# First output projection: four operands loaded and split during the heads, the first result in a tile of its own, the second early sum row loaded 26 matmuls later

## The chip, the core and the metric

The kernel runs on one core of one Trainium2 chip. A core has TensorE (PE, matrix products into PSUM banks), VectorE (DVE), ScalarE (ACT), GpSimd (POOL) and SyncE (SP, which issues DMA transfers and waits for their conditions). The engines run at the same time and wait for each other by semaphores; each one takes its own instructions in order. The metric is device time in microseconds (us) of one execution.

## What is computed

One decoder layer on 1024 tokens of width 1024 in float32. The parts that matter here, cut from the reference:

```python
u = x * (1.0 + sc1) + sh1
proj = u @ w_in[l]
qa, ka, va, dq, dk, dv, z, b_raw, a_raw, g_a, g_b = _split_in(proj)
y_a = _sliding_window_attention(qa, ka, va, sinks[l]) @ w_oa[l]
y_b = _gated_deltanet(dq, dk, dv, z, b_raw, a_raw, ...) @ w_ob[l]
mixed = (jax.nn.sigmoid(g_a) * y_a + jax.nn.sigmoid(g_b) * y_b) @ w_out[l]
x = _layer_norm(ALPHA * x + (1.0 + gt1) * mixed, ln1_g[l], ln1_b[l])
...
```

The window attention has 16 heads. The gated delta rule has 8 heads of 128 channels, each a chain over 8 blocks of 128 tokens. "The first output projection" is the product with `w_oa`. Behind the layer norm follows a squared-ReLU MLP.

## The kernel before

**Products.** Every large float32 product runs as three products of rounded parts: an operand is split into a high part (ACT copies it into a rounded type) and a low part (DVE subtracts the high part from the source). A split costs one instruction on ACT and one on DVE (helper `split_s`, lines 218 to 220: the copy at 219, and `lag` matmuls later the subtraction at 220).

**Order.** The order of PE, ACT and DVE is written out by hand. `at(p, f)` puts a step at matmul number `p`, `after(n, f)` puts it `n` matmuls behind the current one; `count[0]` counts the large matmuls, and before each of them `run_events` emits the steps that are due. `vec` and `act` do the same but move a step into windows that the chain of a head leaves free. SP and POOL are not in this order: a planner places their transfers by when tiles and data are ready in its own reckoning, and each of the two queues then runs in that order and waits at its head.

**Stages.** `Q0` (line 685) is where the heads of the delta rule begin: 24 units of 48 matmuls (line 1436: products for q, v and the gate `gb`) run from `Q0` to `OA` (line 1328, 1152 matmuls later), and the steps of the heads stand between these matmuls. Head `h` runs from `R0 + 120 h`, with `R0 = Q0 + 160` (line 960): `hd_load` brings its matrices, `hd_z` (line 1131) and `hd_x` (1141) complete the inverse of its triangular blocks from the tiles L21 and T1 (`hd_solved`, 1089), and `hd_a`, `hd_b`, `hd_c` are the chain. `hd_x` of a head also runs `hd_z` of the next one into the same bank. `hd_norm` and `hd_out` (1261, 1281) finish a head and store it in `og_d`.

**The sums for the projection.** The projection is a seven-product scheme on quarters (Winograd's form of Strassen's), done for pairs of feature blocks. Its moving operands are the quarters 11, 21 and 22 of the attention output (`attn_d`) and the sums T1 to T4 (`at_d`). The rows of sums are made from `attn_d` by `ts_load`, four steps `ts_step` on DVE (line 1340) and two stores. Rows 0 and 1 are made early (`ts_early`, line 1349) in the two `gate` tiles of `gpool`, rows 2 and 3 near the end of the heads in four tiles of the pool `pc` (`ts_late`). Behind row 1, `ada_open` takes the two gate tiles for loads of `w_ada` (line 1040), 64 of them, each with an add on DVE.

**Operands.** `q_load` (1371) brings half an operand into a raw tile, `q_split` (1379) splits it into a tile named by `HOME`. Operands 11 and T2 are loaded at the end of the heads into the four tiles `late`; the other five (`REST`, line 1433) come through three raw tiles `or` of the pool `p2`, which `open_p2` (1461) opens at `OA + 8` in the space of the pools `pc` and `pce`: it can be used only when all that was in them is done, the last head's store in `og_d` included. `o_load`, `o_op` and `o_sum` (1390 to 1416) bring blocks of `w_oa`, form the sums of these that the seven products need, and split them, at the places of the list `OPS` (1420).

**Projection.** Line 1544 runs 28 products of 12 matmuls from `OA`: for the pairs 0 and 1 in the order 1, 6, 7, 4, then 2, 5, 3, and for the pairs 2 and 3 the other way round. Products 1, 6, 7 and 4 of a pair add up in one bank (`mm`), and so do 5 and 3 (`b`). What stands in a bank between two products is copied out by ACT (`o_part`, line 1506) or added to an earlier copy by DVE (`o_full`, line 1511), before PE may go on in that bank. The copies are in tiles `t` of `p2` (six of them, line 1500); each is stored to `ta_d` by POOL when it is complete, and then its tile is free. `y_load` (1518) fetches them again for the next stage.

Of the kernel before, what the change touches and what calls it, by code (L numbers as in the profile page):

```python
# [9 lines left out]
F32 = mybir.dt.float32  # L10
# [7 lines left out]
P = 128  # L18
D = 1024
S = 1024  # L20
KT = D // P  # L21
NT = S // P
HALF = 512
# [11 lines left out]
def hybrid_layer_kernel(ctx: ExitStack, tc: tile.TileContext,  # L35
                        x, c, w_ada, b_ada, w_in, conv_w, a_log, dt_bias, sinks, dn_norm_w,
                        w_oa, w_ob, w_out, ln1_g, ln1_b, w_ff1, b_ff1, w_ff2, b_ff2,
                        ln2_g, ln2_b, out, dbg=None):
    nc = tc.nc
    x, c, out = x[0], c[0], out[0]  # L40
# [160 lines left out]
    def at(p, f, *args):  # L201
        order[0] += 1
        heapq.heappush(events, (p, order[0], f, args))

    def after(n, f, *args):
        at(count[0] + n, f, *args)
# [728 lines left out]

    pce_pool = tc.tile_pool(name="pce", bufs=1)
    pce = pce_pool.__enter__()
    pc = pc_pool = None
    TTs = []

    def open_pc():
        nonlocal pc, pc_pool
        pb_pool.__exit__(None, None, None)
        vhl_pool.__exit__(None, None, None)
        kp_pool.__exit__(None, None, None)
        pc_pool = tc.tile_pool(name="pc", bufs=2, side="right")
        pc = pc_pool.__enter__()
        for i in range(2):
            TTs.append(pc.tile([P, NT, P], F32, name=f"TT{i}", bufs=1))
            V.memset(TTs[i][64:128, :, 0:64], 0.0)  # L950
# [27 lines left out]
    def vec(lag, cost, f, *args):  # L978
        q = window("V", count[0] + lag, cost)
        at(q, f, *args)  # L980
        return q
# [67 lines left out]
    def ada_load(i, f, k):  # L1049
        w, lo = ada["w"][i % 3], ada_cols_of(f)  # L1050
        nc.sync.dma_start(out=w, in_=w_ada[k * P:(k + 1) * P, lo:lo + HALF])
        q = vec(36, 3.3, ada_add, w, k)
        if k == KT - 1:
            at(q + 7, ada_part, f)

# [26 lines left out]
        after(4, put)  # L1082

    items = [(f, k) for f in range(KT) for k in range(KT)]
    at(Q0 + 112, ada_open)
    for i, (f, k) in enumerate(items):
        at(Q0 + 120 + 14 * i, ada_load, i, f, k)

    def hd_solved(h):
        d = heads[h]  # L1090
# [204 lines left out]
    def gb_done(i):  # L1295
        ts = []

        def done(half, pt):
            t = big4("gz", shape=[P, HALF])
            A.activation(out=t, in_=pt, func=AF.Copy)  # L1300
            nc.sync.dma_start(out=gb_d[i, :, halves[half]], in_=t)
        return done

    for h in range(8):
# [23 lines left out]
    OA = L0 + 48  # L1328
# [20 lines left out]
    def ts_early(k):  # L1349
        tiles = [gpool.tile([P, S], F32, tag="gate", name="ts") for _ in range(2)]  # L1350
        ts_load(k, tiles)
        after(22, ts_step, k, tiles, 0)

    late = []

# [4 lines left out]
            vec(22 + 14 * i, 3.3, ts_step, 2 + i, late[2 * i:2 * i + 2], 0)  # L1360

    at(Q0 + 6, ts_early, 0)
    at(Q0 + 58, ts_early, 1)
    at(R0 + 7 * PER + 2, ts_late)

    QUAD = {"11": (attn_d, 0, 0), "21": (attn_d, 4, 0), "22": (attn_d, 4, 1),
# [14 lines left out]
        quad[name, j] = [(big, big2)[pool].tile([P, 2, HALF], F32R, tag=f"{c}{i + j}", name="q" + c) for c in "hl"]  # L1381
        split_s(*quad[name, j], qraw[name, j], 5)

    for n, (name, j) in enumerate((a, j) for a in ("11", "T2") for j in range(2)):
        at(OA - 66 + n, lambda name, j, n: q_load(name, j, late[n]), name, j, n)
        at(L0 + 8 + 6 * n, q_split, name, j)

    wraw, wop, opn = {}, {}, [0]

# [14 lines left out]
    def o_sum(i, what):  # L1404
# [10 lines left out]
        else:  # L1415
            sub(V, f2h, f2h, f1l)

    at(L0 - 24, o_load, 0, 0)
    at(L0 - 20, o_load, 0, 1)
    OPS = [(-48, 0, "a0"), (-42, 1, "a0"), (-36, 0, "+b"), (-35, 0, "+g0"), (-30, 1, "+b"), (-29, 1, "+g0"),  # L1420
# [9 lines left out]
    for pair in (2, 3):  # L1430
        at(OA + 97, o_load, 1, pair)

    REST = [(n, j) for n in ("T3", "T4", "21", "T1", "22") for j in range(2)]
    RSPLIT = (30, 34, 38, 56, 60, 64, 80, 84, 88, 104)

    for kind, h in units_h:
        if kind == "q":
# [59 lines left out]
    ot = {}  # L1497

    def o_tile(i, c):
        ot[i, c] = p2.tile([P, HALF], F32, tag="t", name="t", bufs=6)  # L1500
        return ot[i, c]

    def o_put(i, c):
# [14 lines left out]
    def y_load(f):  # L1518
        sg = gpool.tile([P, S], F32, tag="gate", name="sg")
        nc.gpsimd.dma_start(out=sg, in_=gb_d[f])  # L1520
        ga = p2.tile([P, S], F32, tag="or", name="ga", bufs=3)
        nc.gpsimd.dma_start(out=ga, in_=ga_d[f])
        ta = [p2.tile([P, HALF], F32, tag="t", name="ta", bufs=6) for _ in range(2)]
        for half in range(2):
            nc.gpsimd.dma_start(out=ta[half], in_=ta_d[f, :, halves[half]])
        ygate[f] = sg, ga, ta
        after(22, lambda: A.activation(out=ga, in_=ga, func=AF.Sigmoid))
        after(28, lambda: A.activation(out=sg, in_=sg, func=AF.Sigmoid))
        for half in range(2):
            after(30 + 4 * half, lambda half: V.tensor_tensor(out=ta[half], in0=ta[half], in1=ga[:, halves[half]],  # L1530
                                                               op=ALU.mult), half)

    at(OA + 7 * 48 - 24, y_load, 0)

    PRODUCT = {1: ("a0", "11", "A", True), 2: ("a4", "21", "B", True), 3: ("g4", "22", "C", False),
               4: ("b4", "T4", "A", False), 5: ("b0", "T1", "C", True), 6: ("g0", "T2", "A", False),
# [7 lines left out]
    for i, m in turns:  # L1544
        w, mv, ab, begin = PRODUCT[m]
        if begin:
            tag = {"A": "mm", "B": "a", "C": "b"}[ab]
            obank[i, ab] = psum(tag, {"mm": 3, "a": 2, "b": 2}[tag])
        pt = obank[i, ab]
        for k in range(4):  # L1550
            for x_ in range(3):
                run_events(count[0])
                t, (qh, ql) = wop[i, w], quad[mv, k // 2]
                lw, r = ((0, qh), (0, ql), (1, qh))[x_]
                T.matmul(pt, lhsT=t[:, lw, k, :], rhs=r[:, k % 2, :], start=begin and k == 0 and x_ == 0,  # L1555
                         stop=k == 3 and x_ == 2, skip_group_check=True)
                count[0] += 1
        e = count[0] + 1
        c = {1: 0, 2: 0, 6: 1, 3: 1, 7: 3, 5: 3, 4: 2}[m]
        if m == 4:  # L1560
            at(e if i > 1 else OA + (128, 152)[i], o_part, i, c, pt, True)
        else:
            at(e, o_part if (m in (1, 6, 7)) == (i < 2) else o_full, i, c, pt)

# [33 lines left out]
    def open_pe():  # L1598
        nonlocal pe, pe_pool, gt1, parts
        p2_pool.__exit__(None, None, None)  # L1600
        gp_pool.__exit__(None, None, None)
        pe_pool = tc.tile_pool(name="pe", bufs=2, side="right")
        pe = pe_pool.__enter__()
        gt1 = pe.tile([P, D], F32, tag="gx", name="gt1", bufs=1)
        row(gt1, gt_d[0])
        parts = pe.tile([P, NT, 2, 6], F32, name="parts", bufs=1)
        for i, name in enumerate(("11", "21", "22")):
            tiles = [[big2.tile([P, 2, HALF], F32R, tag=f"{c}{2 * i + j}", name=f"u{name}{c}") for j in range(2)]
                     for c in "hl"]
            U[name, "t"] = tiles  # L1610
            U[name] = [[t[k // 2][:, k % 2, :] for k in range(4)] for t in tiles]
        for name, k0, u in (("T1", 0, 1), ("T2", 4, 1), ("T3", 0, 0), ("T4", 4, 0)):
            U[name] = [[t[k0 + k].rearrange("p (j u c) -> p j u c", j=4, u=2)[:, :, u, :] for k in range(4)]
                       for t in (mh, ml)]
# [673 lines left out]
```

## Time and profile before

| what | us |
|---|---|
| median of 3 runs | 1829.96 (1828.35 to 1831.01) |
| the profiled execution | 1830.16 |
| its span, first to last instruction | 1828.5 |
| PE busy in the span | 1791.9 |
| mean granted clock of PE | 0.992 |

A line of the timeline gives start, duration, engine, source line, operation, the tiles written and read, and in square brackets how long the engine had been idle and what released it. Engines with a q are sequencers; SPq lines are issues of DMA transfers. A line of the waits gives who waited for whom: total, times, longest. A line of the windows gives the stretch, its length, the busy time of PE, weight loads (PEld), DVE, ACT and POOL with their instruction counts, the granted clock, the share of the DMA engines and GB/s.

### The profile page before, as it was taken

Reading aid. Unit: us, or ns where it says so; the run is one execution under the profiler, and the core shown is the slowest. Engines: PE = TensorE matmul, PEld = TensorE weight load, DVE = VectorE, ACT = ScalarE, POOL = GpSimd, SP = SyncE. Lnnn points to the kernel's source line nnn. Section 1 sums busy time; section 2 is a strip of 40 time slices with the busy share of each in tenths; the row PEclk is TensorE's granted clock in tenths of the full one; section 3 lists DMA queues with packets and bytes.
Section 4 is the critical chain, followed back from the end, with each engine's and each line's share of the span. In section 5 each row is a group of like instructions: output and inputs, shape, how many; then the busy total and the mean of one; then the engine's idle time right before and its main releaser. Section 6 shows DMA issues by size and latency. Waiting matters only on the chain.

```text
span 1828.5 us, 26402 instructions
## 1 busy us (share of the span) xinstructions
PE 1791.9 (98%) x9136; PEld 1506.9 (82%) x9137; DVE 1300.8 (71%) x2430; ACT 1044.5 (57%) x2363; POOL 318.8 (17%) x482
## 2 busy tenths in 40 slices
PE   8999999999998999999988999999999999999998
PEld 6988888888886888888877888888888888888887
DVE  7688688888855567767567455788777766576697
ACT  4699678888864556555465332466555554434341
POOL 0233234453340011101001210001222220000000
PEclk8999999999999999999999999999999999999999
DMA  9656722232267556565666754358888879855671
GB/s 280 202 199 207 225 67 96 65 111 70 73 221 241 131 181 189 169 184 161 227 215 197 257 167 150 120 163 297 307 290 274 278 274 385 277 184 184 198 263 46
DMA packets 270903, 357.66 MB, mean 196 GB/s; under 512 B 27201, under 2 KB 172306, under 8 KB 270514
## 3 DMA queue, kind: packets, MB, share of 16 engines
q1 hardware_dynamic: 230898, 231.81, 40.2%
q0 software_dynamic: 31728, 107.39, 17.5%
q10 hardware_dynamic: 8144, 16.78, 2.6%
q8 instruction: 72, 1.18, 0.3%
q14 instruction: 61, 0.50, 0.1%
HBM read 242.93 MB, written 110.90 MB: 194 GB/s over the span
## 4 chain that ended last, share of the span: by engine, by line
PE 43%; DVE 2%; DMA 2%; ACT 2%; issue 1%; ACTq 0%; SPq 0%; DVEq 0%; POOLq 0%
PE mm L2149 8%; PE mm L2209 7%; PE mm L262 5%; PE a L2209 4%; PE b L2149 4%; PE b L2209 4%; PE a L2149 3%; PE mm L1778 2%; PE c L2209 2%; PE a L1778 1%; PE mm L1555 1%; PE b L1555 1%; PE c L1778 1%; PE c L2149 0%; DMA or<-at_d 0%
## 5 line engine op out<-in xcount | busy, mean ns | idle before, releaser
L262 PE MATMUL mm<-uh,wh 128*128 128x512 f32 x800 | 320.3, 400 | 0.0
L262 PE MATMUL mm<-uh,wl 128*128 128x512 f32 x800 | 319.8, 400 | 0.0
L262 PE MATMUL mm<-ul,wh 128*128 128x512 f32 x800 | 319.2, 399 | 0.0
L220 DVE TENSOR_TENSOR sp<-sraw,sp 128x1024 fp32r<-128x1024 f32 x112 | 132.7, 1219 | 75.7 <-ACT sp L219 75.7
L219 ACT ACTIVATE sp<-sraw 128x1024 fp32r<-128x1024 f32 x112 | 112.6, 1054 | 120.9 <-PE b L2209 75.4
L262 PEld LDWEIGHTS mm<-uh,wh 128*128 128x128 f32 x800 | 151.0, 189 | 26.5
L262 PEld LDWEIGHTS mm<-ul,wh 128*128 128x128 f32 x800 | 151.1, 189 | 26.2
L262 PEld LDWEIGHTS mm<-uh,wl 128*128 128x128 f32 x800 | 151.1, 189 | 26.1
L2209 PE MATMUL mm<-sp 128*128 128x512 f32 x528 | 135.9, 389 | 0.0
L2209 PEld LDWEIGHTS mm<-sp 128*128 128x128 f32 x528 | 98.8, 188 | 20.4
L2209 PE MATMUL a<-sp 128*128 128x512 f32 x336 | 92.2, 389 | 0.0
L825 DVE CUSTOM_DVE_ANT_0 nscore<-a,amask,nsink 128x256 f32<-128x256 f32 (+1 forms) x128 | 54.5, 463 | 44.8 <-PE a L818 44.5
L1234 ACT ACTIVATE vn<-a,brk 128x128 f32<-128x128 f32 x64 | 23.6, 369 | 99.8 <-PE a L1232 99.7
L2209 PE MATMUL b<-sp 128*128 128x512 f32 (+1 forms) x336 | 79.6, 374 | 0.0
L2209 PEld LDWEIGHTS a<-sp 128*128 128x128 f32 x336 | 63.1, 188 | 13.1
L237 DVE TENSOR_TENSOR wl<-wr,wh 128x1024 fp32r<-128x1024 f32 x56 | 69.0, 1231 | 3.4 <-ACT wh L233 3.4
L836 POOL TENSOR_TENSOR sm<-sm 128x256 f32<-128x256 f32 x56 | 51.5, 919 | 104.8 <-ACT sm L832 73.8
L2209 PEld LDWEIGHTS b<-sp 128*128 128x128 f32 x336 | 60.3, 188 | 11.2
L220 DVE TENSOR_TENSOR wl<-fraw,wh 128x1024 fp32r<-128x1024 f32 x43 | 52.5, 1221 | 19.7 <-ACT wh L219 19.6
L832 ACT ACTIVATE sm<-nscore,stat 128x257 f32<-128x257 f32 (+1 forms) x128 | 62.0, 487 | 2.7 <-DVE stat L825 2.5
L219 ACT ACTIVATE wh<-fraw 128x1024 fp32r<-128x1024 f32 x43 | 44.9, 1054 | 31.0 <-PE b L2149 25.1
L877 POOL TENSOR_SCALAR_AFFINE_SELECT pl<-ph 128x512 fp32r<-128x512 f32 x56 | 53.7, 960 | 41.7 <-DVE ph L870 38.1
(577 smaller groups left out, 4761.2 us busy)
## 6 DMA issues: line engine op xcount, KB each, us to landing
wr<-in_w_in_dram SPq DMA_DIRECT2D x60, 512.0 KB, 3.6
sraw<-hf_d SPq DMA_DIRECT2D x54, 512.0 KB, 4.4
adaw<-in_w_ada_dram SPq DMA_DIRECT2D x74, 256.0 KB, 4.9
fraw<-in_w_ff_dram SPq DMA_DIRECT2D x32, 512.0 KB, 5.1
sraw<-wt_d SPq DMA_DIRECT2D x32, 512.0 KB, 4.5
hf_d<-t ACTq DMA_DIRECT2D x48, 256.0 KB, 3.6
wt_d<-wx POOLq DMA_DIRECT2D x48, 256.0 KB, 4.0
sraw<-in_w_ff_dram SPq DMA_DIRECT2D x22, 512.0 KB, 7.4
```

Source lines behind the costliest of these rows:

```text
L219: A.activation(out=hi, in_=src, func=AF.Copy)
L220: after(lag, lambda: V.tensor_tensor(out=lo, in0=src, in1=hi.bitcast(F32), op=ALU.subtract))
L237: V.tensor_tensor(out=hl[1], in0=raw, in1=hl[0].bitcast(F32), op=ALU.subtract)
L262: T.matmul(ts[half], lhsT=w[:, k, :], rhs=xx[k][:, sl], start=k == 0 and m == 0, stop=k == KT - 1 and m == 2)
L825: V.tensor_tensor_reduce(out=ns[:, i, 1:1 + W], in0=sc[:, i * 2 * P:i * 2 * P + W], in1=amask[:, mo:mo + W], scale=-1.0, scalar=nsink[:, 2 ...
L832: A.activation(out=sm[:, i, 0:1 + W], in_=ns[:, i, 0:1 + W], func=AF.Exp, scale=-1.0, bias=st[:, i:i + 1], accum_out=st[:, 2 + i:3 + i])
L836: G.tensor_tensor(out=sm[:, :, 1 + P:1 + 2 * P], in0=sm[:, :, 1:1 + P], in1=sm[:, :, 1 + P:1 + 2 * P], op=ALU.add)
L877: G.affine_select(out=flat4(part), in_=flat4(full), pattern=[[0, 4], [1 if odd else -1, P]], compare_op=ALU.is_ge if odd else ALU.is_gt, f ...
L1555: T.matmul(pt, lhsT=t[:, lw, k, :], rhs=r[:, k % 2, :], start=begin and k == 0 and x_ == 0, stop=k == 3 and x_ == 2, skip_group_check=True)
L1778: T.matmul(pt, lhsT=m[k][:, tok], rhs=w[:, k % 2, :], start=k == 0 and w is wh and m is mh, stop=k == KT - 1 and m is ml)
L2149: T.matmul(pt, lhsT=a[:, kk, :], rhs=b[k], start=begin and k == 0 and x_ == 0, stop=k == 3 and x_ == 2, skip_group_check=True)
L2209: T.matmul(to, lhsT=a[:, f, t * P:(t + 1) * P], rhs=b[:, f, lo:up], start=(begin or own) and s % NS == 0 and f == 0 and x_ == 0, stop=s % ...
```

## The change

- Row 1 of the early sums is loaded at `Q0 + 84` instead of `Q0 + 58`; its first sum stands 40 matmuls behind that instead of 22, and row 0's 30 instead of 22. `ada_open` and the `w_ada` loads start 56 and 52 matmuls later, 13 matmuls apart instead of 14, with the add 33 behind the load instead of 36.
- The stores of `gb` are issued by ACT instead of SP.
- Operands T3 and T4 are loaded together with 11 and T2, into a tile of `pc` and three of `pce`, and split from `OA - 10` on. The raw tiles of `p2` then bring 21, T1 and 22, split at other places.
- The blocks of `w_oa` for the pairs 0 and 1 are loaded 30 and 32 matmuls earlier; their first sums and splits (a0, b, g0) stand 26 to 39 matmuls earlier, b4 of pair 0 stands 13 earlier.
- A new pool `yo`, opened before `pc`, holds one tile `t0`, for the results (0,0), (0,2), (2,0) and (2,2) one after another; `p2` has five tiles `t` instead of six.
- The copies of product 4 stand at `OA + 150, 176, 326, 346` instead of 128, 152 and right behind the product (325 and 337), and `y_load(0)` 5 matmuls later.

```diff
--- before.py
+++ after.py
@@ -935,14 +935,16 @@
 
     pce_pool = tc.tile_pool(name="pce", bufs=1)
     pce = pce_pool.__enter__()
-    pc = pc_pool = None
+    pc = pc_pool = yo = yo_pool = None
     TTs = []
 
     def open_pc():
-        nonlocal pc, pc_pool
+        nonlocal pc, pc_pool, yo, yo_pool
         pb_pool.__exit__(None, None, None)
         vhl_pool.__exit__(None, None, None)
         kp_pool.__exit__(None, None, None)
+        yo_pool = tc.tile_pool(name="yo", bufs=1, side="right")
+        yo = yo_pool.__enter__()
         pc_pool = tc.tile_pool(name="pc", bufs=2, side="right")
         pc = pc_pool.__enter__()
         for i in range(2):
@@ -1049,7 +1051,7 @@
     def ada_load(i, f, k):
         w, lo = ada["w"][i % 3], ada_cols_of(f)
         nc.sync.dma_start(out=w, in_=w_ada[k * P:(k + 1) * P, lo:lo + HALF])
-        q = vec(36, 3.3, ada_add, w, k)
+        q = vec(33, 3.3, ada_add, w, k)
         if k == KT - 1:
             at(q + 7, ada_part, f)
 
@@ -1082,9 +1084,9 @@
         after(4, put)
 
     items = [(f, k) for f in range(KT) for k in range(KT)]
-    at(Q0 + 112, ada_open)
+    at(Q0 + 168, ada_open)
     for i, (f, k) in enumerate(items):
-        at(Q0 + 120 + 14 * i, ada_load, i, f, k)
+        at(Q0 + 172 + 13 * i, ada_load, i, f, k)
 
     def hd_solved(h):
         d = heads[h]
@@ -1298,7 +1300,7 @@
         def done(half, pt):
             t = big4("gz", shape=[P, HALF])
             A.activation(out=t, in_=pt, func=AF.Copy)
-            nc.sync.dma_start(out=gb_d[i, :, halves[half]], in_=t)
+            A.dma_start(out=gb_d[i, :, halves[half]], in_=t)
         return done
 
     for h in range(8):
@@ -1349,7 +1351,7 @@
     def ts_early(k):
         tiles = [gpool.tile([P, S], F32, tag="gate", name="ts") for _ in range(2)]
         ts_load(k, tiles)
-        after(22, ts_step, k, tiles, 0)
+        after((30, 40)[k], ts_step, k, tiles, 0)
 
     late = []
 
@@ -1360,7 +1362,7 @@
             vec(22 + 14 * i, 3.3, ts_step, 2 + i, late[2 * i:2 * i + 2], 0)
 
     at(Q0 + 6, ts_early, 0)
-    at(Q0 + 58, ts_early, 1)
+    at(Q0 + 84, ts_early, 1)
     at(R0 + 7 * PER + 2, ts_late)
 
     QUAD = {"11": (attn_d, 0, 0), "21": (attn_d, 4, 0), "22": (attn_d, 4, 1),
@@ -1381,9 +1383,17 @@
         quad[name, j] = [(big, big2)[pool].tile([P, 2, HALF], F32R, tag=f"{c}{i + j}", name="q" + c) for c in "hl"]
         split_s(*quad[name, j], qraw[name, j], 5)
 
-    for n, (name, j) in enumerate((a, j) for a in ("11", "T2") for j in range(2)):
-        at(OA - 66 + n, lambda name, j, n: q_load(name, j, late[n]), name, j, n)
-        at(L0 + 8 + 6 * n, q_split, name, j)
+    def q_first():
+        spare = late + [pc.tile([P, S], F32, tag="Re", name="qr", bufs=1),
+                        pce.tile([P, S], F32, tag="vT", name="qr"),
+                        pce.tile([P, S], F32, tag="qT", name="qr", bufs=3),
+                        pce.tile([P, S], F32, tag="qT", name="qr", bufs=3)]
+        for n, t in enumerate(spare):
+            q_load(("11", "T2", "T3", "T4")[n // 2], n % 2, t)
+
+    at(OA - 66, q_first)
+    for n, p in enumerate((-42, -36, -30, -22, -10, -4, 2, 7)):
+        at(OA + p, q_split, ("11", "T2", "T3", "T4")[n // 2], n % 2)
 
     wraw, wop, opn = {}, {}, [0]
 
@@ -1415,10 +1425,10 @@
         else:
             sub(V, f2h, f2h, f1l)
 
-    at(L0 - 24, o_load, 0, 0)
-    at(L0 - 20, o_load, 0, 1)
-    OPS = [(-48, 0, "a0"), (-42, 1, "a0"), (-36, 0, "+b"), (-35, 0, "+g0"), (-30, 1, "+b"), (-29, 1, "+g0"),
-           (-14, 0, "g0"), (-8, 1, "g0"), (-2, 0, "b4"), (6, 0, "+d"), (10, 0, "d"), (2, 1, "b4"), (12, 1, "+d"), (16, 1, "d"),
+    at(L0 - 56, o_load, 0, 0)
+    at(L0 - 50, o_load, 0, 1)
+    OPS = [(-76, 0, "a0"), (-70, 1, "a0"), (-64, 0, "+b"), (-61, 0, "+g0"), (-58, 1, "+b"), (-55, 1, "+g0"),
+           (-52, 0, "g0"), (-47, 1, "g0"), (-15, 0, "b4"), (6, 0, "+d"), (10, 0, "d"), (2, 1, "b4"), (12, 1, "+d"), (16, 1, "d"),
            (18, 0, "a4"), (26, 0, "+g4"), (28, 0, "b0"), (40, 1, "a4"), (48, 1, "+g4"), (50, 1, "b0"),
            (86, 0, "g4"), (90, 1, "g4"),
            (118, 2, "a4"), (122, 2, "+b"), (126, 2, "b0"), (130, 3, "a4"), (134, 3, "+b"), (138, 3, "b0"),
@@ -1430,8 +1440,8 @@
     for pair in (2, 3):
         at(OA + 97, o_load, 1, pair)
 
-    REST = [(n, j) for n in ("T3", "T4", "21", "T1", "22") for j in range(2)]
-    RSPLIT = (30, 34, 38, 56, 60, 64, 80, 84, 88, 104)
+    REST = [(n, j) for n in ("21", "T1", "22") for j in range(2)]
+    RSPLIT = (52, 58, 64, 70, 100, 106)
 
     for kind, h in units_h:
         if kind == "q":
@@ -1497,7 +1507,10 @@
     ot = {}
 
     def o_tile(i, c):
-        ot[i, c] = p2.tile([P, HALF], F32, tag="t", name="t", bufs=6)
+        if (i, c) in ((0, 0), (0, 2), (2, 0), (2, 2)):
+            ot[i, c] = yo.tile([P, HALF], F32, tag="t0", name="t0")
+        else:
+            ot[i, c] = p2.tile([P, HALF], F32, tag="t", name="t", bufs=5)
         return ot[i, c]
 
     def o_put(i, c):
@@ -1520,7 +1533,7 @@
         nc.gpsimd.dma_start(out=sg, in_=gb_d[f])
         ga = p2.tile([P, S], F32, tag="or", name="ga", bufs=3)
         nc.gpsimd.dma_start(out=ga, in_=ga_d[f])
-        ta = [p2.tile([P, HALF], F32, tag="t", name="ta", bufs=6) for _ in range(2)]
+        ta = [p2.tile([P, HALF], F32, tag="t", name="ta", bufs=5) for _ in range(2)]
         for half in range(2):
             nc.gpsimd.dma_start(out=ta[half], in_=ta_d[f, :, halves[half]])
         ygate[f] = sg, ga, ta
@@ -1530,7 +1543,7 @@
             after(30 + 4 * half, lambda half: V.tensor_tensor(out=ta[half], in0=ta[half], in1=ga[:, halves[half]],
                                                                op=ALU.mult), half)
 
-    at(OA + 7 * 48 - 24, y_load, 0)
+    at(OA + 7 * 48 - 19, y_load, 0)
 
     PRODUCT = {1: ("a0", "11", "A", True), 2: ("a4", "21", "B", True), 3: ("g4", "22", "C", False),
                4: ("b4", "T4", "A", False), 5: ("b0", "T1", "C", True), 6: ("g0", "T2", "A", False),
@@ -1558,7 +1571,7 @@
         e = count[0] + 1
         c = {1: 0, 2: 0, 6: 1, 3: 1, 7: 3, 5: 3, 4: 2}[m]
         if m == 4:
-            at(e if i > 1 else OA + (128, 152)[i], o_part, i, c, pt, True)
+            at(OA + (150, 176, 326, 346)[i], o_part, i, c, pt, True)
         else:
             at(e, o_part if (m in (1, 6, 7)) == (i < 2) else o_full, i, c, pt)
 
@@ -1598,6 +1611,7 @@
     def open_pe():
         nonlocal pe, pe_pool, gt1, parts
         p2_pool.__exit__(None, None, None)
+        yo_pool.__exit__(None, None, None)
         gp_pool.__exit__(None, None, None)
         pe_pool = tc.tile_pool(name="pe", bufs=2, side="right")
         pe = pe_pool.__enter__()
```

## The prediction

> **What bounds the kernel now.** I read the page first, then busy time in windows, then what TensorE (PE) waited for, then the timelines of each queue around those waits.
>
> ```profile
> span 1828.5 us, 26402 instructions
> PE 1791.9 (98%) x9136; PEld 1506.9 (82%) x9137; DVE 1300.8 (71%) x2430; ACT 1044.5 (57%) x2363; POOL 318.8 (17%) x482
> 550.00:575.00 25.00, 18.05 (x94) 14.66 (x93) 10.46 (x16) 6.30 (x11) 1.12 (x2) 0.88 0.96 309
> 575.00:600.00 25.00, 23.39 (x147) 19.35 (x147) 16.31 (x34) 14.18 (x46) 1.17 (x2) 0.99 0.54 157
> 975.00:1000.00 25.00, 19.10 (x75) 15.66 (x76) 17.94 (x29) 14.67 (x27) 2.69 (x5) 0.86 0.36 124
> PE b L1167 <- ACT Z L1139: 6.9, 1, 6.9
> PE b L1148 <- ACT junk L1171: 1.5, 1, 1.5
> PE b L1555 <- DVE t L1334: 6.0, 1, 6.0
> PE mm L1555 <- ACT t L1507: 4.4, 3, 2.1
> PE b L1286 <- DVE o L1271: 0.2, 1, 0.2
> ```
>
> PE is busy 98% of the span; only the 36.6 us in which it is idle, and slow clock behind a long wait, can be won. Two places matter here: 550 to 600 us, where the heads begin, and 925 to 1000, the first output projection. The waits name 6.9 and 1.5 in the first; 0.2, three that add to 4.4, and 6.0 in the second. In both the granted clock falls (0.88, 0.86).
>
> The first place, link by link (SP, VectorE, ScalarE, PE):
>
> ```profile
> 549.76 1.58 SPq L1347 DMA_DIRECT2D at_d<-ts  x2
> 551.38 1.76 SPq L1104 DMA_DIRECT2D kT<-kt_d  x1
> 563.47 1.49 SPq L1338 DMA_DIRECT2D ts<-attn_d  x2
> 566.01 0.99 SPq L1095 DMA_DIRECT2D L<-l_d  x1
> 572.20 0.92 SPq L1347 DMA_DIRECT2D at_d<-ts  x2
> 573.17 0.66 SPq L1096 DMA_DIRECT2D T<-t_d  x1
> 567.19 0.69 DVE L1331 TENSOR_TENSOR ts<-ts 128x512 f32<-128x512 f32 x1 [9.18 <-DMA ts<-attn_d]
> 571.61 0.63 ACT L1027 ACTIVATE vT<-vT 128x512 f32<-128x512 f32 x1 [14.45 <-DVE vT L1017]
> 565.23 0.39 PE L262 MATMUL mm<-uh,wl 128*128 128x512 f32 x1
> 572.56 1.11 PE L1167 MATMUL b<-ident,qT 128*128 128x128 f32 x4 [6.95 <-ACT Z L1139]
> 573.33 0.78 PE L262 MATMUL mm<-uh,wh 128*128 128x512 f32 x1
> 575.60 0.39 PE L262 MATMUL mm<-uh,wl 128*128 128x512 f32 x1
> 576.29 0.40 PE L262 MATMUL mm<-uh,wl 128*128 128x512 f32 x1
> 577.02 1.16 PE L1183 MATMUL b<-qT,kT 128*128 128x128 f32 x8
> 580.20 0.63 PE L1138 MATMUL b<-T,L 64*64 64x64 f32 x16
> DMA to landing us min/median/max: 2.3/6.4/7.4
> ```
>
> The stores of the first early row go from 549.76 and free its two gate tiles only at about 563.4: the DMA is at 0.96. Until then the queue of SyncE (SP) holds the second row's loads. VectorE (DVE) meets that row's sums at count Q0+80 of the matmuls and sits 9.18 us. Behind it, in order, stand two taps of vT; behind these on ScalarE (ACT) the SiLU (14.45 idle) and the copy of Z; without that copy PE has no bank for its transposes at Q0+120.
>
> The second place:
>
> ```profile
> 941.17 0.60 ACT L1507 ACTIVATE t<-mm 128x512 f32<-128x512 f32 x1 [3.40 <-DMA og_d<-sz]
> 945.07 1.06 ACT L219 ACTIVATE qh<-or 128x1024 fp32r<-128x1024 f32 x1 [1.26 <-DMA or<-at_d]
> 953.99 1.06 ACT L219 ACTIVATE qh<-or 128x1024 fp32r<-128x1024 f32 x1 [1.99 <-DMA or<-attn_d]
> 976.48 0.60 ACT L1507 ACTIVATE t<-mm 128x512 f32<-128x512 f32 x1 [5.69 <-DMA ta_d<-t]
> 939.31 0.39 PE L1555 MATMUL mm<-qh,wo 128*128 128x512 f32 x1
> 948.01 0.50 PE L1555 MATMUL mm<-qh,wo 128*128 128x512 f32 x1 [0.44 <-ACT t L1507]
> 980.90 0.79 PE L1555 MATMUL b<-qh,wo 128*128 128x512 f32 x1 [5.97 <-DVE t L1334]
> 985.73 0.39 PE L1555 MATMUL a<-qh,wo 128*128 128x512 f32 x1
> ```
>
> ACT's first copy out of a bank needs a tile of p2, which opens when the last head's og_d store has landed. Later copies stand behind splits that wait for T3 and 21. The seventh result waits 5.69 us for a t tile, until the first one's store has landed; the adds that PE needs wait behind it.
>
> **The change, part by part.** *The second early row.* Its sums go from count Q0+80 to Q0+124; its loads are written 26 matmuls later. I expect SP to issue them where it does now: the gate tiles hold them, and SP isn't bound to the written place (kT of head 1 is written at Q0+162 and goes at 551.38, 13.9 us before PE is at Q0+120). So they land near 567 to 570 as now, but DVE comes to them only at Q0+124, near 567. It is free at 558.0 (567.19 less 9.18); two taps of 0.7, the SiLU and Z are done by 561, and PE passes 565.5 without the 6.95. What is late next is the product Z of head 1 at Q0+130, which needs two L and two T loads. PE is there at 565.5 + 0.6 (half of 1.11, which ran at half clock) + 10 x 0.23 (575.60 to 576.29 is three) + 1.16 + 0.5 = 570.0. The first L load goes at 566.01; the three behind it no longer stand behind the row's stores (572.20), and go by 568.9. With the landing row of L (2.3 to 7.4) the last one lands between 571.2 and 576.3; the DMA is still full, so I take 574.5, near the median. Z of head 1 then starts 5.7 before 580.20. This takes the 1.5 along, which stood on a late ACT. A wait of 4.5 is left, and PE may leave it at half clock: after the 6.95 five matmuls from 573.33 to 575.60 took 2.3 instead of 1.15, while none of the waits up to 2.1 cost clock. I take 0.7 of 0 to 1.1. Part: **-5.0**, between -9.0 and -2.8.
>
> The Trainium skill, page "TensorE: Matmul & The Clock Gate", section "Part 1: The HAM clock gate", says that an idle window of about 3.4 us halves the clock until a busy one has passed. By that the wait left over pays in full, an estimate of 0.4 us beyond the sum. The waits of 6.95 and 2.1 in this trace agree; none lies between 2.1 and 5.9.
>
> *The ada loads* start 56 matmuls later, 13 apart instead of 14, with a lag of 33 for 36. Each slot is freed 6 matmuls before its next load, as now, and they end 14 matmuls earlier. I cost them at nothing: DVE does them beside a PE that has no named wait within the heads. If a window for DVE overflows it is tenths, either way.
>
> *The gb stores on ACT's queue* free SP for the eight loads, and add 16 issues to ACT:
>
> ```profile
> 1217.34 1.93 ACT L1701 ACTIVATE rawp<-b,sh,sc 128x256 f32<-128x256 f32 x4 [0.40 <-ACT t L1872]
> L219 ACT ACTIVATE qh<-or x10: 1049/1060/1067, 945.1 to 965.6; 128x1024 fp32r<-128x1024 f32 x10
> L220 DVE TENSOR_TENSOR ql<-or,qh x10: 1224/1225/1226, 946.2 to 966.7; 128x1024 fp32r<-128x1024 f32 x10
> vr<-at_d SPq DMA_DIRECT2D x1, 512.0 KB, 7.3
> 937.14 0.63 ACT L219 ACTIVATE wo<-owr 128x512 fp32r<-128x512 f32 x1 [0.82 <-DVE owr L1331]
> DMA to landing us min/median/max: 2.3/2.3/7.4
> ```
>
> ACT stops for 0.40 behind such an issue (the row follows a store of hf_d). Sixteen on the path would be 6.4, none 0. ACT is busy 57%, and PE has five matmuls between a copy of vn and its use, so I take 0 within the heads, and 0.8 of ACT time for the last two, below. Three sums moved ahead delay one rhs of the last head: **+0.2**, an estimate.
>
> *Four more operands in the heads.* T3 and T4 add four splits (ACT 1.06, about 1.0 back to back; DVE 1.2) ahead of the first copy out of a bank. ACT ends its work there at 937.8 now (941.17 less 3.40). It gets 4.0 more and 0.8 for two issues; two splits of weights move further ahead (-1.2), and its first operand starts about 1.0 earlier: 940.4. Most of the 0.82 idle I leave in, since DVE gets 1.2 more with each split too. The first result has a tile of its own, so its copy runs at once, to 941.0. PE, 0.2 earlier, comes at 939.4. So the gap of 2.1 becomes about 1.5, not nothing: **-0.8** with the 0.2. The loads: the last of the four now (vr) lands at 924.6; four more of 512 KB, 1.7 each at the pace of these, are in by 931.5, and ACT comes to T3 near 932.9.
>
> The copy of the second result needs p2, which opens about 0.4 later than now, at 941.5; PE wants it at 941.0 + 12 x 0.23 = 943.7. The gap of 0.44 (behind the T3 splits) goes: **-0.4**. Operand 21 now comes first into p2's three raw tiles, and T1's second half needs the first of them again: free near 950, landed some 3.8 later, as the first raw tile is now (945.07, from p2's opening), split and copied by 955.5. PE wants that copy at 941.0 + 60 x 0.23 = 954.6. So the third of that wait's gaps, 4.4 - 2.1 - 0.44 = 1.8, becomes 0.9: **-0.9**.
>
> *The first result's tile, five t tiles, the copies at 150, 176, 326 and 346.* Result (0,2) takes the tile of (0,0). That one's last product ends at count 108, near 961; its store leaves at 962.4 and lands 2.3 to 7.4 later, by 969.8 at worst. The copy is due at count 150, 970.5. Nothing then holds ACT, and the 5.97 goes, with the slow clock behind it (12 matmuls from 980.90 to 985.73 in 4.8 instead of 2.7): **-8.1**. The later t tiles are freed ten matmuls or more before they are taken again; if that cover fails ACT stops, as it does now.
>
> **Sum**: -5.0 + 0.2 - 0.8 - 0.4 - 0.9 - 8.1 = -15.0. The profiled execution took 1830.16 us (1.7 of it outside the span), which gives 1815.2; it lies 0.2 above the median of 1829.96, so **1815.0**.
>
> **The rivals.** *No wait is left at Z of head 1*: SP puts the L and T loads ahead of the held row. Then the transposes five matmuls later wait about 1.8 for DVE's sums, and the part is -8.6: 1811.4. For it: the row is written later. Against it: SP's order follows what is ready.
>
> *The wait only moves*: SP keeps the row's stores ahead of T, as now (572.20 before 573.17), and they wait for sums that come later; T lands at 578 again. The part is -0.5: 1819.5.
>
> *The first result's tile doesn't help*: its store lands after 970.5, ACT stops at count 150 as now, and the 8.1 are lost: 1823.1. Against it: 7.4 is the longest landing there. Both of the last two: 1827.6.
>
> *Slower*: the loads of T3 and T4 land late. ACT takes its work in order, so each microsecond after 932.9 delays the first copy, and PE, by as much. It decides from 948 on, where the 15 us are used up; landing at 953 gives 1835. Against it: the 931.5 above.
>
> **Chances.** Forecast 0.50, no wait left 0.17, the wait moves 0.15, the tile doesn't help 0.06, both 0.06, slower 0.06. A measurement of this kernel can tell about 0.2% (3.7 us) from no change. Faster by more: the first four, 0.88; within it: "both", 0.06; slower: 0.06. The range 1809 to 1823 takes in the bounds of the forecast's terms, no wait left and the wait that moves: 0.82.
>
> **What would show it.** Right: the 9.18 and 14.45 in front of the taps and the SiLU are gone, PE doesn't wait for Z's copy, and waits 3 to 6 at Z of head 1 instead; ACT's first copy goes without a wait for og_d, to be done near 941; no split of T3 or T4 behind a DMA; PE has a gap of 1 to 2 after the 24th projection matmul and none of 6 near 970. Wrong: DVE idle again at the second row, T landing at 578, ACT idle in front of T3, or a copy that waits for ta_d.

## The result, and the profile after

The changed kernel takes 1817.89 us (median of 4 runs, 1815.92 to 1820.11) beside 1829.66 for the kernel before in the same comparison: a ratio of 0.9936, 95% interval 0.9919 to 0.9953, or 11.8 us. Put on a chip again, it gave 0.9928 (0.9916 to 0.9941). The forecast was 1815.0 with a range of 1809 to 1823, so it is faster, by 3 us less than forecast. The profiled execution took 1817.67 us.

The page of the changed kernel, then its windows, then what PE waited for between 550 and 1010 us:

```profile
span 1815.9 us, 26384 instructions
PE 1790.4 (99%) x9137; PEld 1506.6 (83%) x9137; DVE 1299.6 (72%) x2430; ACT 1044.9 (58%) x2363; POOL 318.7 (18%) x482
```

```profile
550.00:575.00 25.00, 21.80 (x143) 17.95 (x141) 17.56 (x32) 9.97 (x23) 2.00 (x4) 0.97 0.95 308
575.00:600.00 25.00, 25.00 (x119) 20.91 (x120) 9.32 (x20) 12.36 (x38) 0.53 (x1) 0.89 0.40 127
975.00:1000.00 25.00, 25.00 (x112) 20.69 (x111) 19.27 (x30) 16.90 (x30) 4.94 (x10) 1.00 0.78 263
```

```profile
PE mm L1568 <- ACT t L1520: 3.7, 2, 2.3
PE b L1140 <- DMA T<-t_d: 3.2, 2, 3.0
PE a L1245 <- ACT vn L1236: 0.6, 1, 0.6
PE b L1288 <- DVE o L1273: 0.5, 1, 0.5
```

The waits of 6.9 and 6.0 are gone. In their place stand 3.2 at the product Z of head 1, as forecast in kind, and 3.7 in two pieces in the projection. The second window is the surprise: from 575 to 600 PE has no gap at all (25.00), and yet the granted clock, the number ahead of the DMA share, is 0.89. PE pays for the left wait once more, after it.

The timeline of the changed kernel at the two places (SP's issues, DVE, ACT, PE):

```profile
564.01 1.33 SPq L1340 DMA_DIRECT2D ts<-attn_d  x2
565.91 1.05 SPq L1097 DMA_DIRECT2D L<-l_d  x1
569.27 1.36 SPq L1098 DMA_DIRECT2D T<-t_d  x1
575.64 0.55 SPq L1349 DMA_DIRECT2D at_d<-ts  x1
568.45 0.69 DVE L1333 TENSOR_TENSOR ts<-ts 128x512 f32<-128x512 f32 x1 [1.18 <-DMA ts<-attn_d]
930.39 1.99 ACT L219 ACTIVATE qh<-qr 128x1024 fp32r<-128x1024 f32 x2
937.27 0.57 ACT L1520 ACTIVATE t<-mm 128x512 f32<-128x512 f32 x1
952.49 1.06 ACT L219 ACTIVATE qh<-or 128x1024 fp32r<-128x1024 f32 x1 [4.38 <-DMA or<-at_d]
953.46 0.58 ACT L1520 ACTIVATE t<-mm 128x512 f32<-128x512 f32 x1
566.28 0.48 PE L262 MATMUL mm<-uh,wh 128*128 128x512 f32 x1
573.34 0.35 PE L1140 MATMUL b<-T,L 64*64 64x64 f32 x2 [2.99 <-DMA T<-t_d]
579.78 0.63 PE L262 MATMUL mm<-ul,wh 128*128 128x512 f32 x1
580.50 0.40 PE L262 MATMUL mm<-uh,wh 128*128 128x512 f32 x1
937.90 0.50 PE L1568 MATMUL mm<-qh,wo 128*128 128x512 f32 x1 [1.45 <-ACT t L1520]
954.09 0.50 PE L1568 MATMUL mm<-qh,wo 128*128 128x512 f32 x1 [2.30 <-ACT t L1520]
```

SP issues the second row's loads at 564.01, as before (563.47), and the loads of L and T behind them, no longer behind the row's stores (575.64). DVE idles 1.18 there instead of 9.18. PE passes Q0+120 at 566.28 instead of 573.33 and meets the product Z at 573.34, where the forecast had 574.5. From there to about 580.2 its matmuls take 0.63 instead of 0.40. At the end of the heads ACT splits T3 (930.39) without a wait. In the projection its first copy (937.27) waits for nothing, PE's first gap is 1.45 and the 0.44 is gone. The last gap, 2.30 at OA+84, is longer than forecast: ACT's copy at 953.46 stands behind the split of T1's second half, which waits 4.38 for its load.

To keep places apart, the table splits each profiled execution at four starts of PE matmuls, read from its timeline: from Q0 to Q0+160 (the first place), on to OA (the other heads), and from OA to OA+335 (the projection). Q0 itself lies between 534.95 and 538.39 in these executions and is left out.

| kernel | Q0 to Q0+160 | to OA | to OA+335 | median us | ratio to before (95%) |
|---|---|---|---|---|---|
| before | 52.68 | 344.84 | 90.08 | | |
| changed | 48.87 | 344.93 | 80.86 | 1817.89 | 0.9936 (0.9919 to 0.9953) |
| changed, again | 47.04 | 345.03 | 82.68 | 1817.86 | 0.9928 (0.9916 to 0.9941) |
| row alone | 46.99 | 344.68 | 88.06 | 1823.45 | 0.9963 (0.9951 to 0.9976) |
| changed, row undone | 51.04 | 346.92 | 82.33 | 1823.65 | 0.9963 (0.9950 to 0.9975) |
| changed, no own tile | 49.36 | 345.83 | 85.79 | 1822.07 | 0.9955 (0.9940 to 0.9970) |
| own tile and places alone | 52.01 | 346.01 | 83.62 | 1825.04 | 0.9968 (0.9957 to 0.9979) |
| places alone | 53.30 | 346.43 | 82.76 | 1825.47 | 0.9970 (0.9960 to 0.9981) |
| loads of L and T on ACT | 49.71 | 344.95 | 80.09 | 1818.09 | 0.9927 (0.9915 to 0.9940) |
| Z of head 1 later | 43.60 | 345.52 | 82.30 | 1812.13 | 0.9896 (0.9882 to 0.9909) |
| T1's split later | 48.47 | 345.51 | 78.27 | 1815.61 | 0.9920 (0.9907 to 0.9934) |
| gb stores on SP | 46.34 | 344.07 | 81.48 | 1815.57 | 0.9915 (0.9902 to 0.9929) |
| the last three together | 42.56 | 344.14 | 77.79 | 1808.53 | 0.9878 (0.9864 to 0.9891) |

The stretches come from one execution of each kernel, and those of one kernel vary by 2 us from execution to execution: the code of the projection in "row alone" is that of the kernel before, and it took 2.0 less.

### The profile page after: what moved, and what is told of

Same layout as the page of the kernel before. It is cut to its first block, busy times and chain, and to the rows that moved or that the text cites. A ratio compares the mean times of both kernels' runs of the same rounds, so it can differ in the third digit from the quotient of the medians.

```text
span 1815.9 us, 26384 instructions
## 1 busy us (share of the span) xinstructions
PE 1790.4 (99%) x9137; PEld 1506.6 (83%) x9137; DVE 1299.6 (72%) x2430; ACT 1044.9 (58%) x2363; POOL 318.7 (18%) x482
## 3 DMA queue, kind: packets, MB, share of 16 engines
q8 instruction: 72, 1.18, 0.3%
## 4 chain that ended last, share of the span: by engine, by line
PE 89%; ACT 3%; DVE 2%; DMA 1%; issue 1%; ACTq 0%; SPq 0%; POOL 0%; DVEq 0%; POOLq 0%
PE mm L262 35%; PE mm L2163 8%; PE mm L2223 7%; PE a L2223 4%; PE b L2163 4%; PE b L2223 4%; PE a L2163 3%; PE mm L1792 2%; PE c L2223 2%; PE mm L1568 2%; PE c L892 2%; PE a L1792 1%; PE b L1568 1%; PE mm L192 1%; PE mm L190 1%; PE mm L191 1%
```

## The experiments

### The row alone, and all but the row

The first takes from the change only the second early row and the `w_ada` loads; the second undoes just these.

```diff
-        q = vec(36, 3.3, ada_add, w, k)
+        q = vec(33, 3.3, ada_add, w, k)
-    at(Q0 + 112, ada_open)
+    at(Q0 + 168, ada_open)
-        at(Q0 + 120 + 14 * i, ada_load, i, f, k)
+        at(Q0 + 172 + 13 * i, ada_load, i, f, k)
-        after(22, ts_step, k, tiles, 0)
+        after((30, 40)[k], ts_step, k, tiles, 0)
-    at(Q0 + 58, ts_early, 1)
+    at(Q0 + 84, ts_early, 1)
```

> The kernel before with the second early row and the w_ada loads alone moved; stores of gb stay on SP, the projection is untouched. Theory (the row's part stands by itself and is worth 3.8, since PE starts the product Z of head 1 at half clock behind a wait of 3): 1826 us, the 6.9 on the copy of Z gone, a wait near 3 at Z of head 1 with slow clock behind it, and the 6.0 at the seventh product as before. Rival (the part needs the gb stores off SP: two of them stand ahead of the L and T loads): T lands at 578 again, 1829.

> The changed kernel with the second early row and the w_ada loads back at their old places. Theory (two independent places, 3.8 and 8.7): 1821.5 us, with the 6.9 on the copy of Z back and no 6.0 in the projection. Rival (what the heads gain is swallowed by later waits, so the projection part gives nearly all): 1818 to 1819.

PE's waits with the row alone:

```profile
PE b L1555 <- DVE t L1334: 4.6, 1, 4.6
PE mm L1555 <- ACT t L1507: 4.3, 3, 2.0
PE b L1138 <- DMA T<-t_d: 2.7, 2, 2.5
```

The row stands by itself: the wait for the copy of Z is gone, 2.7 is left at Z of head 1, and the waits of the projection are still there. The gb stores had no part in it, so that rival falls. The row gave 6.8 us by time (0.0037 of 1830), more than the 3.8 of the changed kernel's first profile that the theory had taken; its first stretch is 5.7 shorter than before. Undone, it costs 5.8 (1823.65 less 1817.89). So the two places are independent, and 3.8 was a low draw: the left wait cost less here, for a reason that comes up below.

### Without the first result's tile, and with the tile and the places alone

In the first, all results are again in six tiles `t` of `p2` and the copies of product 4 at their old places, while the four operands are still prepared in the heads. The second puts the tile and the later places into the kernel before.

```diff
-        if (i, c) in ((0, 0), (0, 2), (2, 0), (2, 2)):
-            ot[i, c] = yo.tile([P, HALF], F32, tag="t0", name="t0")
-        else:
-            ot[i, c] = p2.tile([P, HALF], F32, tag="t", name="t", bufs=5)
+        ot[i, c] = p2.tile([P, HALF], F32, tag="t", name="t", bufs=6)
...
-            at(OA + (150, 176, 326, 346)[i], o_part, i, c, pt, True)
+            at(e if i > 1 else OA + (128, 152)[i], o_part, i, c, pt, True)
```

> The changed kernel without the tile t0: all results in six tiles t of p2, the copies of product 4 at their old places, the four operands still loaded and split in the heads. Theory of the prediction (the tile and the later places remove the 5.97 and its slow clock): both come back, and the first copy waits for og_d again: 1817.9 + 8.1 + 2 = 1828. Rival (the operands in the heads make the first result complete 8 us earlier, its store lands near 966, and nothing holds the copy): only the first copy waits for og_d, 1820 to 1820.5.

> The kernel before with the tile t0, five tiles t and the later copies of product 4 alone; T3 and T4 still come through p2. Theory of the prediction (tile and places remove the first gap of 2.1 and the 5.97 with its slow clock): 1830 - 2 - 8 = 1820. Rival (the operands do it; the adds still come late behind splits that wait for their loads): the first gap goes and the 6 stays in some form, 1826 to 1828.

What PE waited for without the tile, then with the tile and the places alone:

```profile
PE mm L1565 <- ACT t L1517: 5.4, 2, 3.3
```

```profile
PE mm L1560 <- ACT t L1512: 3.1, 1, 3.1
PE b L1560 <- DVE t L1336: 1.4, 1, 1.4
```

Without the tile the rival holds, but for its price. The wait of 6 does not come back (no line names DVE's `t`), so what is left of the change removes it. Most likely that is the work done ahead in the heads, the operands and the blocks of `w_oa`, since the row alone leaves 4.6; no run parts these two from each other or from the gb stores. The first result's store left 1.4 us after PE came to OA+108, where its last product ends (967.92 and 969.34), and landed 2.8 later. In the kernel before it left 5.2 after that place (963.89 and 969.08) and took 7.4.

What comes back is the first copy's wait: the last part of the `og_d` store landed at 942.27 and the copy began at 942.41. PE's gap at OA+24 is 3.3 instead of 1.45 (with 1.6 of slow clock behind it: the next 12 matmuls took 4.45 instead of 2.85). By medians the kernel is 4.2 slower than the changed one, though the two intervals overlap, and the execution that was profiled was the slowest of its five (1826.11).

With tile and places alone the theory holds for the 6, which is down to 1.4, but not for the sum: 1825 instead of 1820. The first gap goes, and 3.1 comes at a later copy, behind splits that still wait for T3. So each half of the change takes away most or all of the 6 by itself.

### The later places alone

In the run above, the copy at OA+150 waited 0.35 for the store in `ta_d`, so the tile did not look like the cause. This one changes one line of the kernel before.

```diff
-            at(e if i > 1 else OA + (128, 152)[i], o_part, i, c, pt, True)
+            at(OA + (150, 176, 326, 346)[i], o_part, i, c, pt, True)
```

> The kernel before with nothing changed but the places of the four copies of product 4 (OA+150, 176, 326, 346); no tile t0, T3 and T4 through p2. Theory from the run with tile and places (there the copy at OA+150 waits 0.35 for the store in ta_d, so the place does it): the 6.0 becomes about 1.4, the slow clock behind it goes, the first gap of 2.1 stays, 1830.5 - 6.5 = 1824. Rival (the tile does it): the copy still holds ACT to 976.5 and PE waits near 6 as before, 1830.

ACT's copy and PE's waits in the projection:

```profile
979.64 0.60 ACT L1507 ACTIVATE t<-mm 128x512 f32<-128x512 f32 x1 [1.30 <-DMA ta_d<-t]
PE mm L1555 <- ACT t L1507: 3.9, 3, 2.1
PE b L1555 <- DVE t L1334: 1.0, 1, 1.0
```

The places do it: ACT waits 1.30 instead of 5.69, PE 1.0 instead of 6.0, and the kernel gains 5.5 us (0.0030 of 1830). With the tile on top it gained 5.9: the intervals lie on each other. So the 6 had two sufficient remedies in the change: the places, and what the run without tile and places still held, most likely the work done ahead in the heads. Behind the later places the tile adds nothing to them; the tile at the old places was not run. What the tile pays for is the first copy: its gap of 2.1 is there with the places alone and gone with the tile.

### The loads of L and T on ACT's queue

```diff
+        q = A if h == 1 else nc.sync
         for i in range(2):
-            nc.sync.dma_start(out=L21[half[i]], in_=l21_d[h, :, i::2, :])
-            nc.sync.dma_start(out=T1[half[i]], in_=t_d[h, 0, i::2].rearrange("n a s -> a n s"))
+            q.dma_start(out=L21[half[i]], in_=l21_d[h, :, i::2, :])
+            q.dma_start(out=T1[half[i]], in_=t_d[h, 0, i::2].rearrange("n a s -> a n s"))
```

> The changed kernel with the four L and T loads of head 1 issued by ACT at their place (Q0+94) instead of SP, where they stand behind the held row. Theory (the wait of 3.2 at Z of head 1 and 3.0 of half clock behind it both hang on these loads): T lands before 570, both go, 1817.9 - 6 = 1812. Rival 1 (the wait goes, the slow clock has another cause): 1815. Rival 2 (the DMA is full, the place of the issue doesn't matter): T lands near 573 as now, 1817 to 1819.

ACT's timeline, then PE's waits:

```profile
562.40 0.59 ACTq L1098 DMA_DIRECT2D L<-l_d  x1
563.54 0.60 ACTq L1099 DMA_DIRECT2D T<-t_d  x1
565.12 0.53 ACTq L1098 DMA_DIRECT2D L<-l_d  x1
566.42 0.59 ACTq L1099 DMA_DIRECT2D T<-t_d  x1
567.06 0.38 ACT L1142 ACTIVATE Z<-b 128x256 f32<-128x256 f32 x1 [6.74 <-DMA L<-l_d]
```

```profile
PE b L1186 <- DVE E L1190: 1.5, 1, 1.5
PE b L1151 <- ACT junk L1174: 1.5, 1, 1.5
PE b L1170 <- ACT Z L1142: 1.1, 1, 1.1
```

The wait at Z is gone, and three others add to 4.1 in its place: 1818.09, nothing won. None of the three is longer than 1.5, and yet the granted clock is 0.52 from 574 to 578.

ACT did nothing else from 560.3 (567.06 less 6.74) to 567.06. Its four issues add to 2.3 of that; the rest is waiting ahead of them. By the landings in the trace each issue began within 0.1 us of the landing of an earlier transfer of SP, whose semaphore it uses again: a weight load (landed at 562.30), kT (563.52) and the two stores of the first early row (565.10 and 566.40). So on ACT's queue, too, the loads stood behind the transfers that had held SP, now with ACT behind them; the DMA engines' share was 1.04 from 560 to 567. The last T load was in by 571.98 instead of 573.77. The Trainium skill, page "Trainium Kernel Development and Optimization", section "Key Constraints", says that issuing from several engines saves only the issuing sequencer's time, since all share the same DMA engines. Here the loads came 1.8 earlier, and ACT lost 6.74.

### Z of head 1 later

The product isn't used before Q0+225, so it can wait for its loads behind other matmuls.

```diff
-        if h < 7:
+        if h == 0:
+            after(13, hd_z, 1)
+        elif h < 7:
             hd_z(h + 1, xp)
```

> The changed kernel with the product Z of head 1 13 matmuls later in a bank of its own (it isn't used before Q0+225); the loads are untouched. Theory (13 x 0.23 = 3 of work covers the wait, and a wait under 1 leaves the clock alone): 1817.9 - 3 - 3 = 1812. Rival 1 (slow clock has another cause, the small products): 1815. Rival 2 (the transposes and the products q k behind it, which wait for DVE's sums, are late instead): 1816 to 1818.

PE's waits, then two windows:

```profile
PE mm L1570 <- ACT t L1522: 3.6, 2, 2.1
PE b L1140 <- DVE E L1191: 0.8, 1, 0.8
```

```profile
572.00:576.00 4.00, 3.21 (x28) 2.15 (x27) 3.08 (x8) 2.07 (x10) 0.53 (x1) 1.00 0.72 265
576.00:580.00 4.00, 4.00 (x22) 3.33 (x21) 2.26 (x3) 2.71 (x8) 0.00 (x0) 1.00 1.02 273
```

1812.13, as the theory had it: with a wait of 0.8 the clock stays at 1.00. The same small products run as before, so they are not the cause of the slow clock; the wait ahead of them is.

### T1's split later, and the gb stores back on SP

```diff
-    RSPLIT = (52, 58, 64, 70, 100, 106)
+    RSPLIT = (52, 58, 64, 76, 100, 106)
```

> The changed kernel with the split of T1's second half at OA+76 instead of OA+70, behind the copy that PE waits 2.3 for at OA+84. Theory (that copy stands behind a split whose load lands at 952.47): the 2.3 goes, 1815.6. Rival (the adds and splits behind it on DVE and ACT come later, and a later product waits): 1817 to 1819.

```diff
-            A.dma_start(out=gb_d[i, :, halves[half]], in_=t)
+            nc.sync.dma_start(out=gb_d[i, :, halves[half]], in_=t)
```

> The changed kernel with the gb stores back on SP. Theory (an issue on ACT costs 0.4 of ACT's time, which nothing in the heads feels; two of them stand ahead of the first copy out of a bank): the gap of 1.45 at OA+24 becomes 0.7, 1817.2. Rival (SP's queue, held by waits, delays the operands' loads or T): a split of T3 or T4 behind a DMA or a longer wait at Z of head 1, 1819 to 1822.

PE's waits with T1's split later, and with gb on SP, and ACT at `vn` in the changed kernel:

```profile
PE b L1140 <- DMA T<-t_d: 3.1, 1, 3.1
PE mm L1568 <- ACT t L1520: 1.4, 1, 1.4
```

```profile
PE mm L1568 <- ACT t L1520: 2.3, 2, 2.0
PE b L1140 <- DMA T<-t_d: 2.2, 1, 2.2
PE b L1288 <- DVE o L1273: 0.5, 1, 0.5
```

```profile
910.22 0.33 ACTq L1303 DMA_DIRECT2D gb_d<-gz  x1
910.60 0.37 ACT L1236 ACTIVATE vn<-a,brk 128x128 f32<-128x128 f32 x1 [0.40 <-ACT gz L1302]
```

Behind T1's later split the gap of 2.3 is gone and nothing takes its place: the projection is 2.6 shorter. By time the two kernels' intervals overlap (1815.61 beside 1817.9), so it rests on the profile. The same holds of gb on SP (1815.57). There two things go. The gap at OA+24 is 0.3 (2.3 in all, less the 2.0 at OA+84) instead of 1.45. And the line of `vn` is missing: 0.6 in every profile in which ACT issues these stores (seven of them), in none where SP does (six). The issues on ACT cost some 1.7 us here, where the prediction had 0 within the heads and 0.8 ahead of the first copy. In this execution PE's wait for T fell on Z of head 0 rather than head 1; the edit doesn't touch those loads, and I can't say why.

### The three together, and the changed kernel again

> The changed kernel with three of the edits above together: Z of head 1 13 matmuls later, T1's second half at OA+76, the gb stores on SP. Theory (three different waits, so the gains add: 3 + 3 at Z of head 1, 2.3 at OA+84, 0.9 in the heads and 1.1 at OA+24 from the issues on ACT): 1817.9 - 10 = 1808. Rival (they share one cause, or a wait moves as one goes): no better than the best of them alone, 1812.

> The changed kernel itself once more, on the same chip as the run of all three, so that the two can be compared: 1817.9. If the slow clock behind the wait at Z of head 1 depends on when the wait falls, its length differs from the 7 us of the first profile (4 us in the run with the row alone) while the wait stays near 3.

All that PE waited for from 550 to 1010 with the three together:

```profile
PE b L1290 <- DVE o L1275: 0.5, 1, 0.5
PE mm L1570 <- ACT t L1522: 0.4, 1, 0.4
```

The gains add: 1808.53, 9.3 below the changed kernel on the same chip and 21.7 below the kernel before (ratio 0.9878, 0.9864 to 0.9891). This version beats both.

The changed kernel again had the same waits, 2.7 at Z and 2.5 at OA+84, but other slow clocks. Windows of its first profile, then of the second:

```profile
576.00:580.00 4.00, 4.00 (x13) 3.22 (x12) 0.69 (x1) 1.85 (x10) 0.53 (x1) 0.50 0.88 290
954.00:958.00 4.00, 3.91 (x17) 3.26 (x18) 3.24 (x4) 3.49 (x6) 0.00 (x0) 1.00 0.54 150
```

```profile
576.00:580.00 4.00, 4.00 (x16) 3.27 (x15) 0.69 (x1) 1.69 (x10) 0.53 (x1) 0.72 1.02 297
954.00:958.00 4.00, 4.00 (x12) 3.11 (x12) 1.60 (x2) 1.85 (x3) 0.00 (x0) 0.61 0.93 293
```

In the first, PE is slow for 6.9 us behind Z (573.3 to 580.2) and not at all behind the 2.3 at OA+84. In the second it is slow for 3.5 at each place (574.7 to 578.2, 953.5 to 957.0, where matmuls start 0.43 apart instead of 0.23). What was lost at one place was saved at the other, and the spans are 1815.9 and 1816.2.

## Why the prediction was right, and where it was not

**The second early row** (forecast -5.0): right in mechanism, link by link. SP issues the loads where it did, DVE and ACT are free, and the wait moves to Z of head 1, where it ended 1.2 earlier than forecast and was 3.2 instead of 4.5. The term that failed was the clock: I gave it 0.7 and at most 1.1, from the five slow matmuls behind the 6.95. Half of 6.9 and of 3.5 us of slow clock is 3.4 and 1.7. So the part came out at -3.8 in one execution and -5.6 in the other. The sentence beside the sum that drew on the Trainium skill, page "TensorE: Matmul & The Clock Gate", section "Part 1: The HAM clock gate" (the wait left over pays in full), was nearer than the sum, though its estimate of 0.4 beyond the sum was too small. The rivals "no wait left" and "the wait only moves" both fell: 3.2 is left, and T goes ahead of the row's stores.

**The w_ada loads** (nothing): 344.84 and 344.93 us for the stretch to OA.

**The gb stores on ACT** (0 in the heads, 0.8 ahead of the first copy): the second half was right and is the cause of the 1.45 left at OA+24. The first failed: 0.6 at `vn`, which waits when the issue falls right in front of it. Five matmuls of cover were not enough.

**The first copy and the 0.44** (-0.8, -0.4): the gap of 1.45 was forecast as 1.5; the 0.44 is gone.

**The third gap** (1.8 to 0.9): wrong sign. It is 2.3 and 2.5. T1's load took 5.5 us (issued at 947.01, split from 952.49) where I had taken 3.8 from the first raw tile, and a split that waits holds the copy behind it on ACT.

**The 5.97 and its slow clock** (-8.1): the size was about right (the first profile's projection is 9.2 shorter, 0.7 of it at the first three gaps), the credit wrong. I gave all of it to the first result's tile and the later places, by the landing of that result's store: leaving at 962.4, landed by 969.8, copy due at 970.5. In the changed kernel that is how it goes: PE is at OA+108 at 959.66, the store leaves 1.2 later, and the copy runs at 969.37 without a wait. But with tile and places alone the store left 4.7 behind that place (965.10 and 969.84): its early start comes from the rest of the change, which my sum had at nothing here. The runs show that either this rest or the later places remove most or all of the 6 without the tile. That the sum came out was partly luck: the change held a second remedy for the same wait.

The forecast of 1815.0 missed by 2.9. The first profile has 1.2 of it at the first place (3.8 instead of 5.0) and 1.4 in the third gap (+0.5 instead of -0.9). The rival "slower" fell, since T3 was there when ACT came to it.

## What to carry to other kernels

Count a wait of PE together with the clock behind it: in the changed kernel waits of 2.5 to 3.0 us cost 1.7 to 3.4 more, and one of 2.3 nothing. Move the waiting product behind other matmuls before you try to hasten its load. When a change holds several edits that could each remove a wait, test each alone before you name the cause; and order a queue so that no copy that PE needs stands behind a split that waits for a load.

## What the runs showed of the hardware

Whether the clock falls behind a wait of 2.0 to 2.5 us isn't settled by the length of the wait. The same gap at OA+84 cost nothing behind 2.30 in one execution and 1.7, half of the slow stretch, behind 2.5 in another of the same kernel. With the gb stores on SP it was 1.97, and the granted clock was 0.50 behind it, from 950 to 953. That it depends on when the wait falls fits all of these; no run moved one wait by itself. The Trainium skill, page "TensorE: Matmul & The Clock Gate", section "Part 1: The HAM clock gate", says that the clock follows a free-running window of 3.4 us, so that one kernel's number of slow matmuls at its start differs from run to run. The stretches agree: one window (3.5 and 3.5) or two (6.9). But the waits were shorter than the idle window that the page asks for, and the slow clock came all the same: 1.97 us was enough.

An issue on ACT costs more than its own time. A gb store, 0.33 on the queue, left 0.40 to 0.46 between ACT's instructions, and four loads of 0.5 to 0.6 held the engine for 6.7, most of it in waiting for earlier transfers to land.
